# FFN-out by seven block products, two FFN-in tiles read at once, and block sums kept in DRAM

## The chip, the cores and the metric

One core of one Trainium2 chip runs one layer of a sequence model on 512 tokens of width 1024, batch 1, in float32. The metric is the device time of one execution in microseconds. TensorE is called PE, VectorE DVE, ScalarE ACT, GpSimd POOL; SP and POOL issue the DMA transfers spoken of here. Matrix products are exact to about float32: every operand is split into a high part (float32r, cast by ACT) and a low part (the rest, subtracted by DVE), and every product is three matmuls, high by high, high by low, low by high.

## The reference, cut to what matters

```python
def reference(x, ...):                       # x: (1, 512, 1024), D_FF = 2816
    h = rms_norm(x, norm1_g)
    proj = h @ w_in                          # three token mixers and three gate groups
    ...
    branch_out = einsum('blnc,ncd->blnd', branches, w_branch)
    merged = sum(gates * branch_out, axis=2)
    x = x + merged @ w_out                   # 1024 x 1024
    h2 = rms_norm(x, norm2_g)
    gu = h2 @ w_ffn_in                       # 1024 x 5632
    x = x + (silu(gu[..., :D_FF]) * gu[..., D_FF:]) @ w_ffn_out   # 2816 x 1024
    return x
```

The change touches the last two products and the order of the loads ahead of them.

## The kernel before

Activations lie transposed: features on the 128 partitions, the 512 tokens along the free axis. The input projection, the mixers and the gates take the first 545 us or so and are the same in both kernels. Behind them stand four stages.

**Branch merge** (up to about 612 us). For each of eight feature tiles, three products with `w_branch`, multiplied by the gates that SP fetches back from DRAM. Weights of all plain products come 128x512 at a time ("a piece", 256 KB) into a ring `wr` of three tiles (`Dense.load`, L1228), are cast to `wh` by ACT (L1229) and the rest goes to `wl` on DVE (L1230); `wh` and `wl` are rings of six.

**Out-projection** (612 to 664 us). Eight tiles of `w_out`. Behind each tile `take_res` adds the residual (L1717, DVE), `SevenProducts.take` makes the normed input of the FFN and its block sums (L1339 to L1350), `norm.add` adds squares, and the new residual is stored to DRAM (L1720).

**FFN-in** (to 885.8 us). The class `SevenProducts` does the gate and the up product by a Strassen-Winograd scheme over 2 x 2 blocks: the feature axis is cut in two halves of four 128-row tiles, the tokens in two halves of 256, and the weight blocks are the gate and the up column. Instead of eight block products it needs seven, p1 to p7, each of 4 x 3 matmuls of 256 columns (L1391). A tile of 128 gate and 128 up columns costs 84 matmuls; there are 22 tiles, 1848 matmuls in all. They run in pairs, the pieces of the two tiles alternating: p1 p1 p5 p5 p6 p6 p3 p3 p7 p7 p2 p2 p4 p4. Each tile has its own banks, uses half of each, and its results are read by itself: copies of the banks p1, p5, p6, p7 (ACT), additions of 256 columns (DVE), a 512-wide product with the RMS scale (L1443) and SiLU (L1444), and a split of the 512-wide result to `act` (ACT L256, DVE L257).

Of a tile's four weight blocks g0, s, g1, u1, SP loads each (L1377), POOL adds one on top of s and later one on top of g0 (L1375, DMAs that accumulate), and DVE adds g0 and then g1 to s (L1415). The raw blocks lie in a ring of twelve: six tiles that are taken from the slots of the out-projection, which come free late, three new tiles `sp_raw0` to 2, and the three of `wr`. `run` makes a piece (sum, cast, subtract) five pieces ahead of its matmuls: behind the matmuls of piece i in program order come its bank's reads, and ahead of them the split of piece i+5.

**FFN-out** (to 1005.3 us). Plain products: eight tiles of 22 x 3 = 528 matmuls of 512 columns in all (L1301 to L1303). Behind each tile `take_out` multiplies by the RMS scale (L1751), adds the residual read back from DRAM (L1752), and stores the tile (L1753).

The engines run their own instruction streams in program order and wait on semaphores; a scheduler orders the instructions of one stream by readiness in its own estimate when the program is built, so rows of one engine differ somewhat from the code's order.

## Time and profile before

| | us |
|---|---|
| median of 3 runs | 1011.73 |
| lowest, highest | 1007.13, 1014.23 |
| profiled execution, its own time | 1011.66 |
| span in its trace | 1009.9 |
| PE busy | 970.1 (96%) |
| DVE busy | 754.3 (75%) |
| ACT busy | 473.5 (47%) |

The span runs from the first to the last instruction on the core; 1.8 us of the execution's own time lie outside it. Busy shares are averages over stages of different kinds, so that the profile has to be read by stage: a window's row gives each engine's busy time and number of instructions in a stretch, the TensorE clock that was granted, the mean busy share of the 16 DMA engines and the rate. The records of a few matmuls are missing from the trace.

### The profile page before, as it was taken

How to read it: one execution, taken by the hardware profiler on the slowest of the kernel's cores; microseconds unless marked ns; L12 is line 12 of the kernel's file. 1: busy time of each engine (PE TensorE's matmuls, PEld its weight loads, DVE VectorE, ACT ScalarE, POOL GpSimd, SP SyncE). 2: the span in 40 equal slices, each digit the busy share in tenths (PEclk: the TensorE clock that was granted, in tenths of full speed). 3: DMA queues.
4: the chain of work that ended last, by engine and by line, in shares of the span. 5: the costliest groups of instructions: out<-in, count | busy, mean ns of one | idle time of the engine just before them, and what ended most of it. 6: DMA issues, size and time to landing. Idle time of an engine off the chain costs nothing.

```text
span 1009.9 us, 17883 instructions
## 1 busy us (share of the span) xinstructions
PE 970.1 (96%) x6416; PEld 824.2 (82%) x6416; DVE 754.3 (75%) x1941; ACT 473.5 (47%) x978; POOL 143.3 (14%) x176
## 2 busy tenths in 40 slices
PE   7989999899999999999999999989999999999998
PEld 5777777676779777888887788879999999988886
DVE  6899676789994789977867655679989998943331
ACT  6534333434342566446446324566666666632220
POOL 2021120422420001000000332011211221000000
PEclk9999899999998999999999999999999999999999
DMA  7325242221431334252448864476776677354440
GB/s 241 116 53 133 64 110 78 84 56 53 100 96 40 95 105 116 84 156 75 154 149 270 273 194 159 138 178 165 151 163 175 152 153 170 79 155 123 131 136 27
DMA packets 105593, 129.95 MB, mean 129 GB/s; under 512 B 45376, under 2 KB 47296, under 8 KB 105504
## 3 DMA queue, kind: packets, MB, share of 16 engines
q1 hardware_dynamic: 99168, 117.28, 38.7%
q0 software_dynamic: 6336, 11.54, 7.4%
q8 instruction: 50, 0.82, 0.3%
q14 instruction: 39, 0.32, 0.1%
HBM read 109.90 MB, written 18.88 MB: 128 GB/s over the span
## 4 chain that ended last, share of the span: by engine, by line
PE 77%; DVE 15%; DMA 3%; ACT 2%; issue 2%; POOL 1%; SPq 0%; DVEq 0%; ACTq 0%; POOLq 0%
PE bank L1391 21%; PE bank L1302 13%; PE bank L1303 13%; PE bank L1301 13%; DVE wl L1230 2%; DMA ar<-in_w_ffn_in 1%; DMA ar<-ymix 1%; PE bank L468 1%; PE bank L479 1%; PE bank L1188 1%; PE bank L262 1%; PE bank L630 1%; PE bank L1285 1%; PE bank L1286 1%; PE bank L1287 1%
## 5 line engine op out<-in xcount | busy, mean ns | idle before, releaser
L1229 ACT CAST wh<-wr 128x512 fp32r<-128x512 f32 x198 | 120.4, 611 | 208.8 <-PE bank L1302 163.6
L1230 DVE TENSOR_TENSOR wl<-wr,wh 128x512 fp32r<-128x512 f32 x198 | 136.8, 693 | 82.8 <-ACT wh L1229 82.3
L1301 PE MATMUL bank<-act_hi,wh 128*128 128x512 f32 x360 | 150.5, 418 | 7.8 <-ACT wh L1229 5.9
L1302 PE MATMUL bank<-act_lo,wh 128*128 128x512 f32 x360 | 149.7, 416 | 0.8 <-DVE act_lo L257 0.7
L1303 PE MATMUL bank<-act_hi,wl 128*128 128x512 f32 x360 | 149.6, 416 | 0.0
L1391 PE MATMUL bank<-sp_t,wh 128*128 128x256 f32 x528 | 97.5, 285 | 1.1 <-ACT ar L1423 0.8
L1391 PE MATMUL bank<-act_hi,wh 128*128 128x256 f32 x352 | 98.0, 278 | 0.0
L1391 PE MATMUL bank<-act_hi,wl 128*128 128x256 f32 x352 | 97.7, 278 | 0.1
L1391 PE MATMUL bank<-act_lo,wh 128*128 128x256 f32 x352 | 97.5, 277 | 0.0
L1301 PEld LDWEIGHTS bank<-act_hi,wh 128*128 128x128 f32 x360 | 70.0, 195 | 22.7 <-ACT wh L1229 5.9
L1391 PEld LDWEIGHTS bank<-sp_t,wh 128*128 128x128 f32 x528 | 82.7, 193 | 1.5 <-ACT ar L1423 1.0
L1302 PEld LDWEIGHTS bank<-act_lo,wh 128*128 128x128 f32 x360 | 70.0, 194 | 16.4 <-DVE act_lo L257 3.5
L1303 PEld LDWEIGHTS bank<-act_hi,wl 128*128 128x128 f32 x360 | 70.0, 194 | 14.4 <-issue 0.6
L1391 PE MATMUL bank<-sp_t,wl 128*128 128x256 f32 x264 | 75.2, 285 | 0.0
L1301 PE MATMUL bank<-act,wh 128*128 128x512 f32 x176 | 68.5, 389 | 0.0
L1302 PE MATMUL bank<-act,wh 128*128 128x512 f32 x176 | 68.5, 389 | 0.0
L1303 PE MATMUL bank<-act,wl 128*128 128x512 f32 x176 | 68.5, 389 | 0.0
L1391 PEld LDWEIGHTS bank<-act_hi,wl 128*128 128x128 f32 x352 | 66.2, 188 | 0.7 <-DVE wl L254 0.7
L1391 PEld LDWEIGHTS bank<-act_hi,wh 128*128 128x128 f32 x352 | 66.4, 189 | 0.3
L1391 PEld LDWEIGHTS bank<-act_lo,wh 128*128 128x128 f32 x352 | 66.4, 189 | 0.0
L253 ACT CAST wh<-ar 128x512 fp32r<-128x512 f32 x79 | 48.2, 622 | 28.1 <-DMA ar<-in_w_ffn_in 18.1
L254 DVE TENSOR_TENSOR wl<-ar,wh 128x512 fp32r<-128x512 f32 x79 | 53.1, 685 | 9.4 <-ACT wh L253 8.9
(491 smaller groups left out, 2217.7 us busy)
## 6 DMA issues: line engine op xcount, KB each, us to landing
wr<-in_w_in SPq DMA_DIRECT2D x88, 256.0 KB, 2.9
ar<-in_w_ffn_in SPq DMA_DIRECT2D x46, 256.0 KB, 3.2
wr<-in_w_ffn_out SPq DMA_DIRECT2D x40, 256.0 KB, 2.7
gate<-ar SPq DMA_DIRECT2D x24, 256.0 KB, 2.4
wr<-in_w_branch SPq DMA_DIRECT2D x24, 256.0 KB, 3.6
ar<-gate SPq DMA_DIRECT2D x24, 256.0 KB, 3.6
ar<-in_w_ffn_in POOLq DMA_DIRECT2D x22, 256.0 KB, 3.9
sp_raw<-in_w_ffn_in SPq DMA_DIRECT2D x21, 256.0 KB, 3.4
```

The source lines that it names most:

```text
L253: nc.scalar.copy(hi, src)
L254: nc.vector.tensor_tensor(lo, src, hi.bitcast(F32), ALU.subtract)
L262: self.nc.tensor.matmul(ps[:, b, :], sq[:, b * P:(b + 1) * P], self.c("sel"), start=True, stop=True)
L468: nc.tensor.matmul(pa[:, c * P:(c + 1) * P], kb[rows, 4 * q + c].rearrange("p a t -> p (a t)"), ar[rows, 4 * q + c].rearrange("p a t -> p ...
L479: nc.tensor.matmul(pt[64:128, w], aam[q][0:64, c, h, 1], uv[0:64, 4 * q + c, h * CH:(h + 1) * CH], start=True, stop=True)
L630: nc.tensor.matmul(pu[:, 0:P], yt[:, c0:c0 + 2].rearrange("p c t -> p (c t)"), ts, start=True, stop=True)
L1229: nc.scalar.copy(wh, raw)
L1230: nc.vector.tensor_tensor(wl, raw, wh.bitcast(F32), ALU.subtract)
L1301: nc.tensor.matmul(ps, wh[:, j], hi(k), start=k == 0, stop=False)
L1302: nc.tensor.matmul(ps, wh[:, j], lo(k), start=False, stop=False)
L1303: nc.tensor.matmul(ps, wl[:, j], hi(k), start=False, stop=k == nk - 1)
L1391: nc.tensor.matmul(ps, w[x][:, c], b(y, j), start=first and j == js[0] and n == 0, stop=last and j == js[-1] and n == 2, skip_group_check= ...
```

## The change

1. **FFN-out by seven products.** The 22 k-tiles of the activations become two halves of 11, the tokens two halves of 256, and the output columns are taken in two groups of four tiles, g = 0 and 1. A group has three units, over 4, 4 and 3 k-tiles (chunks c); its seven banks accumulate over the three. 2 x 2 x 7 x 11 x 3 = 924 matmuls of 256 columns take the place of 528 of 512. The results of a group are read behind its third unit only, by DVE and ACT for two output tiles at once (`unit_out`), with the scale and the residual.
2. **Two tiles of FFN-in in one bank.** A pair of tiles is one unit; its two products lie in the two halves of a bank and are read by instructions of 512 columns. SiLU and the split are 1024 wide.
3. **Block sums of the activations.** Behind a unit's results DVE makes four block sums of 256 columns; one stays in SBUF, three are written to DRAM (384 KB per unit) and read back by `fetch` for FFN-out, 512 KB (or 384 KB) at a time, twelve times, through the two work buffers `k[1]` and `n[1]`, and split there by ACT and DVE.
4. **Raw blocks** lie in a ring of eleven: `sp_raw0` to 7, new tiles of their own, and the three of `wr`. No slot of the out-projection is used. The second s of a unit is loaded apart from the other head blocks, when piece 8 of the unit before is made.
5. `w_ffn_in` and `w_ffn_out` are arranged by blocks ahead of the launch, `x2dr` is one DRAM tile, the RMS scale has a place of its own.

```diff
@@ SevenProducts.__init__
-        self.raws, self.turn = None, 0
+        self.raws = [E.spool.tile([P, KB * P], F32, name=f"sp_raw{i}") for i in range(8)] + dense.rings["wr"][0]
+        self.turn = 0
+        a = [x for x, _ in E.tail]
+        self.k = [x[:, 0:5 * self.N].rearrange("p (s n) -> p s n", n=self.N) for x in a[0:2]]
+        self.n = [a[2][:, i * 2 * T:(i + 1) * 2 * T].rearrange("p (s n) -> p s n", n=self.N) for i in range(2)]
+        self.sums = a[0][:, 5 * self.N:8 * self.N].rearrange("p (s n) -> p s n", n=self.N)
+        self.sdr = E.dpool.tile([3, P, KF // 2, self.N], F32, name="sp_sums")
...
@@ FFN-in, reads of a unit (two tiles; releases of banks left out)
+        def r2():
+            V.tensor_tensor(ka, ka, bank("p2"), ALU.add)
+            for k, t in ((ka, a), (kb, b)):
+                V.tensor_tensor(k, k, self.R[:, t].unsqueeze(1).broadcast_to([P, 2, N]), ALU.mult)
+            nc.scalar.activation(K[:, 0:4], K[:, 0:4], AF.Silu)
+        def r4():
+            V.tensor_tensor(ka, ka, bank("p1"), ALU.mult)
+            V.tensor_tensor(kb, kb, nb, ALU.mult)
+            V.tensor_tensor(K[:, 4], K[:, 1], K[:, 0], ALU.subtract)
+            V.tensor_tensor(S[:, 1], K[:, 3], K[:, 0], ALU.subtract)
+            V.tensor_tensor(S[:, 0], K[:, 3], K[:, 4], ALU.add)
+            V.tensor_tensor(S[:, 2], S[:, 0], K[:, 2], ALU.subtract)
+            E.split(K[:, 1:5].rearrange("p s n -> p (s n)"), arenas[j][:, 0:4 * N], arenas[j][:, 4 * N:8 * N], -1.0)
+            nc.sync.dma_start(self.sdr[:, :, j].rearrange("s p n -> p s n"), S)
...
+    def fetch(self, i, c):
+        t = (self.k[1], self.n[1])[self.fetched % 2][:, 0:k]
+        nc.sync.dma_start(t, self.sdr[i, :, 4 * c:4 * c + k])
+        hi, lo = self.place(i, c)
+        E.split(t.rearrange("p s n -> p (s n)"), hi[:, 0:k * N], lo[:, 0:k * N], 1.0 if i == 0 else -1.0)
...
@@ FFN-out, reads of a group (r7 without the releases of banks; r1, r5, r6, r2, r4 in the same manner)
+        def r7():
+            V.tensor_tensor(na, kb, bank("p7"), ALU.add)
+            V.tensor_tensor(kb, kb, nb, ALU.add)
+            V.tensor_tensor(kb, kb, bank("p3"), ALU.add)
+            V.tensor_tensor(nb, nb, na, ALU.add)
+            for v, xx, t, sign, q in ((kb, x[0][:, :, 1], b, 1.0, 0), (nb, x[1][:, :, 1], b, -1.0, 1)):
+                scaled(v, t, sign)
+                V.tensor_tensor(v, v, xx, ALU.add)
+                done(v, q, t)
...
+    HEAD, FOURTH = (("g0", 0), ("s", 0), ("g0", 1)), ("s", 1)
+    REST = (("g1", 0), ("u1", 0), ("g1", 1), ("u1", 1))
...
@@ run
+                if k % n == 0 and k:
+                    self.fill(k // n, *self.REST)
+                    self.fill(k // n + 1, *self.HEAD)
                 pieces[k][0]()
+                if k % n == 8:
+                    self.fill(k // n + 1, self.FOURTH)
...
+    for u, k, i, c in ((n - 1, 1, 0, 0), (n - 1, 4, 1, 0), (n - 1, 6, 2, 0), (n, 0, 0, 1), (n, 2, 1, 1), (n, 6, 2, 1),
+                       (n + 1, 0, 0, 2), (n + 1, 2, 1, 2), (n + 1, 6, 2, 2), (n + 2, 6, 2, 0), (n + 3, 6, 2, 1),
+                       (n + 4, 6, 2, 2)):
+        between.setdefault(14 * u + 2 * k + 1, []).append(lambda i=i, c=c: sp.fetch(i, c))
-    for d in range(KD):
-        dense(A["w_ffn_out"][d], KF, lambda k: ah[k], lambda k: al[k], take_out(d))
```

How instructions move is shown at three places.

SP's stream in the branch merge before (L1228 loads weights, L1695 fetches gates, L1377 loads raw blocks of FFN-in), just behind `sp_raw0` and 1:

```order
L1377 DMA sp_raw2_5979<-in_w_ffn_in 128x512
L1695 DMA ar13_14_82<-gate_60_270 128x512
L1228 DMA wr_16_102<-in_w_branch 128x512
L1695 DMA ar12_13_81<-gate_68_278 128x512
L1228 DMA wr_19_114<-in_w_branch 128x512
L1695 DMA ar12_13_81<-gate_52_262 128x512
L1228 DMA wr_22_135<-in_w_branch 128x512
L1695 DMA ar11_12_80<-gate_61_271 128x512
L1228 DMA wr_16_102<-in_w_branch 128x512
```

The other raw blocks of the first pairs stand further down in that stream, behind the loads of the out-projection:

```order
L1377 DMA wr_19_114<-in_w_ffn_in 128x512
L1720 DMA x2_207_5676<-ar13_14_82 128x512
L1377 DMA ar12_13_81<-in_w_ffn_in 128x512
L1377 DMA ar13_14_82<-in_w_ffn_in 128x512
L1720 DMA x2_208_5677<-ar13_14_82 128x512
L1377 DMA ar12_13_81<-in_w_ffn_in 128x512
L1377 DMA ar11_12_80<-in_w_ffn_in 128x512 x2
```

The same place of the merge in the changed kernel (L1234 weights, L1809 gates, L1382 raw blocks):

```order
L1382 DMA sp_raw2_5674<-in_w_ffn_in 128x512
L1382 DMA sp_raw3_5675<-in_w_ffn_in 128x512
L1234 DMA wr_16_102<-in_w_branch 128x512
L1809 DMA ar13_14_82<-gate_60_270 128x512
L1382 DMA sp_raw4_5676<-in_w_ffn_in 128x512
L1382 DMA sp_raw5_5677<-in_w_ffn_in 128x512
L1234 DMA wr_19_114<-in_w_branch 128x512
L1809 DMA ar12_13_81<-gate_68_278 128x512
L1809 DMA ar12_13_81<-gate_52_262 128x512
L1382 DMA sp_raw6_5678<-in_w_ffn_in 128x512
L1234 DMA wr_22_135<-in_w_branch 128x512
L1382 DMA sp_raw7_5679<-in_w_ffn_in 128x512
```

All eight raw blocks of the first unit, in eight tiles of their own, are now loaded within the merge.

ACT's stream at the end of FFN-in before (L1229 casts pieces of FFN-out, L1436 copies a bank, L1444 is SiLU, L256 casts the result):

```order
L1229 CAST wh_211_5990<-wr_19_114 128x512
L1436 COPY ar11_12_80<-bank5_88 128x256
L1229 CAST wh_17_103<-wr_22_135 128x512
L1436 COPY ar11_12_80<-bank1_84 128x256
L1229 CAST wh_20_115<-wr_16_102 128x512
L1444 ACTIVATE ar12_13_81<-ar12_13_81 128x512
L1229 CAST wh_23_137<-wr_19_114 128x512
L1229 CAST wh_25_143<-wr_22_135 128x512
L1444 ACTIVATE ar13_14_82<-ar13_14_82 128x512
L256 ACTIVATE act_223_6054<-ar12_13_81 128x512
L1229 CAST wh_27_148<-wr_16_102 128x256
L256 ACTIVATE act_223_6054<-ar13_14_82 128x512
```

ACT's stream in the last FFN-in unit of the changed kernel (L259 casts a piece, L1479 and L1456 copy banks, L262 to `sp_t0` or `act_hi` casts a fetched sum, L1464 is SiLU):

```order
L1479 COPY ar11_12_80<-bank3_86 128x2x256
L259 CAST wh_25_143<-wr_16_102 128x512
L262 ACTIVATE sp_t0_5668<-ar13_14_82 128x1024
L259 CAST wh_27_148<-wr_22_135 128x512
L259 CAST wh_203_5989<-sp_raw0_5672 128x512
L259 CAST wh_17_103<-sp_raw2_5674 128x512
L1456 COPY ar13_14_82<-bank3_86 128x512
L259 CAST wh_20_115<-sp_raw1_5673 128x512
L259 CAST wh_23_137<-sp_raw3_5675 128x512
L262 ACTIVATE act_hi_91<-ar12_13_81 128x1024
L262 ACTIVATE act_hi_91<-ar13_14_82 128x1024
L1464 ACTIVATE ar11_12_80<-ar11_12_80 128x1024
```

Three of the casts of fetched sums stand here among those of the pieces, and a fourth, of the first fetch, in the row just ahead of the L1479 copy; two stand ahead of SiLU.

DVE's stream at the end of FFN-out before (L1230 makes a piece, L1751 and L1752 are the results of a tile):

```order
L1230 TENSOR_TENSOR wl_18_104<-wr_22_135,wh_17_103 128x512
L1230 TENSOR_TENSOR wl_21_116<-wr_16_102,wh_20_115 128x512
L1230 TENSOR_TENSOR wl_24_140<-wr_19_114,wh_23_137 128x512
L1230 TENSOR_TENSOR wl_26_144<-wr_22_135,wh_25_143 128x512
L1751 TENSOR_TENSOR ar11_12_80<-bank5_88,ar12_13_81 128x512
L1230 TENSOR_TENSOR wl_28_149<-wr_16_102,wh_27_148 128x256
L1752 TENSOR_TENSOR ar12_13_81<-ar12_13_81,ar11_12_80 128x512
L1751 TENSOR_TENSOR ar13_14_82<-bank1_84,ar12_13_81 128x512
L1752 TENSOR_TENSOR ar13_14_82<-ar13_14_82 128x512
```

DVE's stream in the changed kernel where group 0 ends and group 1 begins (L1546 to L1562 read results of group 0, L260 makes a piece):

```order
L260 TENSOR_TENSOR wl_21_116<-sp_raw3_5675,wh_20_115 128x512
L1547 TENSOR_TENSOR ar11_12_80<-ar11_12_80,bank5_88 128x2x256
L1549 TENSOR_TENSOR ar13_14_82<-ar13_14_82 128x2x256
L1521 SCALAR_TENSOR_TENSOR ar11_12_80<-ar11_12_80,ar12_13_81 128x2x256
L1521 SCALAR_TENSOR_TENSOR ar13_14_82<-ar13_14_82,ar12_13_81 128x2x256
L1552 TENSOR_TENSOR ar11_12_80<-ar11_12_80,ar12_13_81 128x2x256
L1552 TENSOR_TENSOR ar13_14_82<-ar13_14_82 128x2x256
L1556 TENSOR_TENSOR ar11_12_80<-ar11_12_80,bank2_85 128x2x256
L1521 SCALAR_TENSOR_TENSOR ar13_14_82<-ar13_14_82,ar12_13_81 128x2x256
L1521 SCALAR_TENSOR_TENSOR ar11_12_80<-ar11_12_80,ar12_13_81 128x2x256
L1562 TENSOR_TENSOR ar13_14_82<-ar13_14_82 128x2x256
L1559 TENSOR_TENSOR ar11_12_80<-ar11_12_80,ar12_13_81 128x2x256
L260 TENSOR_TENSOR wl_24_140<-sp_raw5_5677,wh_23_137 128x512
```

Eleven result instructions of 512 columns stand in a row between the third and the fourth piece of group 1; at the end of the program the same results (15 instructions with those around them) are DVE's last rows.

## Rows read from the trace of the kernel before

**Rows 1.** The profile's page: busy time of each engine, and the chain that ended last.

```profile
PE 970.1 (96%) x6416; PEld 824.2 (82%) x6416; DVE 754.3 (75%) x1941; ACT 473.5 (47%) x978; POOL 143.3 (14%) x176
PE 77%; DVE 15%; DMA 3%; ACT 2%; issue 2%; POOL 1%; SPq 0%; DVEq 0%; ACTq 0%; POOLq 0%
```

**Rows 2.** Busy time by window: length, engines, granted clock, DMA share, GB/s.

```profile
650.00:676.00 26.00, 21.73 (x125) 18.65 (x124) 20.65 (x43) 15.89 (x35) 5.39 (x6) 0.98 0.69 167
695.00:855.00 160.00, 160.00 (x1376) 159.82 (x1375) 144.54 (x276) 102.98 (x212) 27.81 (x32) 1.00 0.70 162
890.00:1000.00 110.00, 110.00 (x487) 91.09 (x486) 34.92 (x55) 24.07 (x41) 0.00 (x0) 1.00 0.40 120
```

**Rows 3.** The chain of waits from 640 us: start, length, what.

```profile
661.18 4.40 DMA ar<-in_w_ffn_in
...
675.00 10.28 PE bank L1391 x73
...
885.76 0.23 PE bank L1301
...
1005.24 0.24 PE bank L1303
```

**Rows 4.** What PE waited for, 640 to 690 us: total, times, longest.

```profile
PE bank L1303 <- DVE wl L1230: 2.0, 1, 2.0
PE bank L1542 <- DVE ar L1529: 1.2, 1, 1.2
PE bank L1391 <- ACT ar L1423: 0.8, 1, 0.8
PE bank L1391 <- ACT ar L1429: 0.2, 1, 0.2
```

**Rows 5.** PE by window at the start of FFN-in: busy, count, granted clock, DMA.

```profile
674.00:676.00 2.00, 1.77 (x12) 0.77 0.36 41
676.00:678.00 2.00, 2.00 (x11) 0.50 0.83 186
678.00:680.00 2.00, 2.00 (x17) 0.88 0.84 238
```

**Rows 6.** The casts of FFN-in's results: the second one (timeline), all 22 (by tile).

```profile
692.36 0.64 ACT L256 ACTIVATE act<-ar 128x512 fp32r<-128x512 f32 x1 [0.84 <-DVE ar L1450]
...
L256 ACT ACTIVATE act<-ar x22: 616/632/635, 690.5 to 886.9; 128x512 fp32r<-128x512 f32 x22
```

**Rows 7.** DVE groups by shape in FFN-in, 695 to 855 us: busy, mean ns, idle.

```profile
L254 DVE TENSOR_TENSOR wl<-ar,wh 128x512 fp32r<-128x512 f32 x60 | 40.3, 684 | 4.8 <-ACT wh L253 4.4
...
L1438 DVE TENSOR_TENSOR ar<-ar 128x256 f32<-128x256 f32 x16 | 6.7, 418 | 0.0
...
L1415 DVE TENSOR_TENSOR ar<-ar,ar 128x512 f32<-128x512 f32 x9 | 6.1, 681 | 0.0
```

**Rows 8.** DVE's timeline in the out-projection: start, length, instruction.

```profile
658.39 0.68 DVE L1717 TENSOR_TENSOR ar<-ar,bank 128x512 f32<-128x512 f32 x1
658.99 0.68 DVE L1230 TENSOR_TENSOR wl<-wr,wh 128x512 fp32r<-128x512 f32 x1
```

**Rows 9.** ACT groups by shape, 695 to 855 us.

```profile
L1444 ACT ACTIVATE ar<-ar 128x512 f32<-128x512 f32 x16 | 10.1, 633 | 12.6 <-DVE ar L1443 12.6
L1426 ACT COPY ar<-bank 128x256 f32<-128x256 f32 x17 | 6.2, 365 | 0.1
```

**Rows 10.** DMA issues of the page: queue, count, KB each, median us to landing.

```profile
sp_raw<-in_w_ffn_in SPq DMA_DIRECT2D x21, 256.0 KB, 3.4
...
sp_raw<-in_w_ffn_in POOLq DMA_DIRECT2D x10, 256.0 KB, 4.2
...
ar<-in_w_lora SPq DMA_DIRECT2D x1, 512.0 KB, 5.8
```

**Rows 11.** The timeline at the end of the program.

```profile
1005.08 0.39 PE L1303 MATMUL bank<-act,wl 128*128 128x512 f32 x1
1005.51 0.69 DVE L1751 TENSOR_TENSOR ar<-bank,ar 128x512 f32<-128x512 f32 x1 [13.33 <-PE bank L1303]
1006.23 0.69 DVE L1752 TENSOR_TENSOR ar<-ar 128x512 f32<-128x512 f32 x1
```

More of the change, by code (lines that the diff above doesn't have):

```diff
@@ L1378, in load @@
         return t
-    def split(self, w):
-        d = self.dense
-        hi, lo = d.ring("wh", F32R, WB[1] + 1), d.ring("wl", F32R, WB[1] + 1)
-        self.E.split(w, hi, lo)
-        return hi, lo
-    def matmuls(self, ps, w, b, js, first, last):
-        nc = self.E.nc
-        for j in js:
-            c = slice(j * P, (j + 1) * P)
-            for n, (x, y) in enumerate(((0, 0), (0, 1), (1, 0))):
-                nc.tensor.matmul(ps, w[x][:, c], b(y, j), start=first and j == js[0] and n == 0,
-                                 stop=last and j == js[-1] and n == 2, skip_group_check=True)
@@ L1413, in sum_ @@
-        def sum_(other, after=None):
-            def f():
-                V.tensor_tensor(o["s"], o["s"], o[other], ALU.add)
-                if after:
-                    after()
-                return o["s"]
-            return f
+        K, Nn, S = self.k[j % 2], self.n[j % 2], self.sums
+        ka, kb, na, nb = K[:, 1:3], K[:, 0:4:3], Nn[:, 0:2], Nn[:, 2:4]
+        u = dict(blocks=blocks, h=H, banks={}, own=False, new=True, last=True)
+        bank = lambda name: u["banks"][name].rearrange("p (t n) -> p t n", n=N)
@@ new lines, in unit_out, with block, fill @@
+        u["read"] = dict(p1=r1, p5=r5, p6=r6, p7=r7, p2=r2, p4=r4)
+        return u
+    def block(self, u, i, t):
+        w = u["blocks"][i]
+        n = w.shape[1] // 2
+        return w[:, t * n:(t + 1) * n]
+    def fill(self, i, *keys):
+        if i < len(self.units):
+            u = self.units[i]
+            for name, t in keys:
+                u[name, t] = self.load(self.block(u, dict(g0=0, s=1, g1=3, u1=2)[name], t))
+            for name, t in keys:
+                if name == "s":
+                    self.load(self.block(u, 2, t), u["s", t])
@@ new lines, with begin, run @@
+    HEAD, FOURTH = (("g0", 0), ("s", 0), ("g0", 1)), ("s", 1)
+    REST = (("g1", 0), ("u1", 0), ("g1", 1), ("u1", 1))
+    def begin(self, units):
+        self.units, self.fetched = units, 0
+        self.pieces = [p for u in units for p in self.seven(u)]
+        self.fill(0, *self.HEAD, self.FOURTH, *self.REST)
+        for k in range(self.FIRST):
+            self.pieces[k][0]()
+    def run(self, norm, between):
+        pieces, made, n = self.pieces, self.FIRST, 14
+        self.fill(1, *self.HEAD)
@@ L1522, in add @@
         with E.scope("s"):
-            sq = E.slot("rsq", keep=True)
+            sq = self.into if self.into is not None and self.n == 0 else E.slot("rsq", keep=True)
             E.nc.scalar.activation(sq, x, AF.Square)
@@ L1547, in __call__ @@
             nc.tensor.transpose(pb[:, b * P:(b + 1) * P], w[:, b * P:(b + 1) * P], E.ident)
-        E.free(w, pss)
+        E.free(*([pss] if self.into is not None else [w, pss]))
         return pb
```

272 lines of the change are left out of this document (155 added, 117 removed).

## The prediction

> **What bounds the kernel now.** I read the page first, then the chain of waits, then the windows by stage. The page shows PE busy for 96% of the span and on 77% of the chain that ended last [rows 1]. The windows say that this holds stage by stage: in steady FFN-in PE is busy for all 160 us at full clock, in FFN-out for all 110 [rows 2]. So a matmul less is time less, so long as nothing else becomes late. What could is DVE: 144.5 of 160 us in FFN-in, but only 34.9 of 110 in FFN-out [rows 2]. The one place where PE is not full is the start of FFN-in, 650 to 676 us, with 21.7 of 26 us. There the chain runs through loads of `w_ffn_in`, of which the longest shown holds it for 4.4 us [rows 3], and PE's waits are 2.0, 1.2, 0.8 and 0.2 us [rows 4]. Behind them the granted clock falls to 0.50, the lower of its two levels (1.2 GHz against 2.4), for one window and part of the next two [rows 5]. The program ends with two DVE instructions and a store behind the last matmul [rows 11].
>
> The sum is made against the profiled execution, 1011.66 us, which stands at the median of the runs, 1011.73.
>
> **1. Matmuls of FFN-out: -12.7.** Before: from 885.76 to 1005.47 (the last start plus 0.23) is 119.7 us for 528 matmuls, 0.2267 each [rows 3]. Their price at 256 columns comes from FFN-in: the casts of the second tile of the first and of the last pair start at 692.4 and 886.9, ten units of 168 matmuls later, so 19.45 us a unit and 0.1158 each [rows 6]. 924 x 0.1158 = 107.0. Ends: half of a 512-column one (0.1133) gives 104.7, the 1376 records in 160 us, some missing, give 0.1163 and 107.4 [rows 2]. So -12.2 to -15.
>
> **2. The start of FFN-in: -4.5.** The four waits sum to 4.2 us. In 674 to 680 us PE ran 40 matmuls where 52 would fit at 0.1158; less the 0.2 of waiting this is 1.2 us of clock. Together 5.4. The raw blocks of the first pairs came late since six of their tiles were slots of the out-projection: SP issued them behind its stores. Now eight tiles are free from the merge on, and SP's rows put all eight loads there. What may stay is the way from the last residual through gain, block sums and splits on ACT and DVE to p6 and the RMS matmul (the 1.2 of L1542): four pieces of 12 matmuls, 5.6 us, lie beside it. I leave 0.9. Ends: 0, if that way was the real cause, to -5.4. For the five loads that move ahead of weights and gates in SP's queue during the merge, +0.5 (0 to +1): each is 3.4 us of transfer [rows 10], the ring of three weight tiles being the cover; if that cover is gone, a weight is late by one such load in part.
>
> **3. Steady FFN-in: 0.** By durations of DVE, two tiles took 14 splits and 4 sums at 0.68, twelve reads of 256 columns at 0.42, two scalings and two results at 0.68 [rows 7], 20.1 us. Now: the same splits and sums, 7 reads at 0.68, 4 sums of 256 at 0.42, and a 1024-wide result, 1.22 by adding 0.27 for each 256 columns as between the shapes of these rows: 20.0. ACT: four copies of 365 ns less by pairing, and SiLU and cast of 1024 wide at about 1.17 for pairs of 633 [rows 9]: no more than before. DVE starts instructions 0.60 apart that last 0.68 [rows 8], which is how 20.1 fits in 19.45; what hides all this is PE, and the margin is below 2 us a unit. The stores of sums add 0.4 MB to a unit at a DMA share of 0.70 [rows 2]; nobody waits for them there. Ends: 0, and the second rival.
>
> **4. From FFN-in to FFN-out: +3 (0 to +7).** The fetches work through two buffers that the unit before the last still uses. The first is issued once that unit's results are split, about 5.5 us into the last unit, and takes as long as the nearest transfer of its size, 512 KB in 5.8 us [rows 10]. In ACT's order its cast stands ahead of the copy of p6, ready at six pieces, 8.3 us: ACT, with five casts of pieces queued behind, stands for some 3 us. Five pieces ahead are 7 us of cover, so PE need not see it. The next two fetches stand ahead of SiLU in the same way, and behind SiLU wait the products and p6's split of the first FFN-out unit, with some 4 us left. Thirdly, DVE gets three splits of 1024 more in a unit and a half, 27.9 us of work on 27.6 us of PE. I take 2.5 for this border, and 0.5 for the fetches of the other units, whose buffers are free early.
>
> **5. From group 0 to group 1: +4.2 (+2 to +7).** From the end of p7, DVE has in its order 15 results, 7 splits and 4 sums to the split with which p3 of group 1 can start. Independent ones start 0.60 apart [rows 8], those on the result before 0.72 (1005.51 to 1006.23) [rows 11]: 15 x 0.66 + 11 x 0.605 = 16.6 us. PE has four pieces of 9 matmuls and six of 12 in that time, 12.5. The difference is 4.1, and 0.1 for the step from matmul to DVE. The VectorE page of the Trainium skill (VectorE: DVE Perf Modes, section The DRAIN you can't avoid) says that a next operation does not start until the pipe has emptied, and itself excepts operations that are not held; by that the 26 would cost their durations, 17.8, and this term +5.3. The starts 0.60 apart speak for the lower price. A stall of several us may also take the clock: before, PE's waits at FFN-in's start ended in 1.2 us lost [rows 4, 5], and that is in the upper end. The Trainium skill (TensorE: Matmul & The Clock Gate, section HAM oscillation — how this bites in real kernels) lets gaps of PE that recur lower the clock each time. It speaks against a change that makes two new gaps; at the row's price that would be 2.4 us for both. I count none in the sum, since the wait of 2.0 us alone did not bring the clock down: 0.98 over 650 to 676 us is what the 0.77 of the last two leaves [rows 2, 5].
>
> **6. The tail: +4.3 (+3.5 to +5.5).** Before, 1.45 us of DVE lie behind the last matmul's end (1005.47 to 1006.92) [rows 11]. After, 15 results of 512 columns follow p7's end, 15 x 0.66 = 9.9, beside 4 pieces x 9 x 0.1158 = 4.2 us of PE: 5.7 behind the last matmul. The store that follows is as before.
>
> Sum: -12.7 - 4.5 + 0.5 + 0 + 3 + 4.2 + 4.3 = -5.2: **1006.5 us**. Its own range, from terms 2, 4 and 5, is 1002 to 1011.
>
> **Rivals.**
> - *The borders are cheap.* The start gives all 5.4, the extra loads nothing, FFN-in ends with 0.5, and 2 and 3.5 are paid at the other borders: 1011.66 - 12.7 - 5.4 + 0.5 + 2 + 3.5 = 999.6. For it: PE has five pieces ahead, and DVE is two thirds idle in plain FFN-out. Against it: DVE's order at the group's end is fixed, and shows eleven results in a row.
> - *s comes late in every unit: slower.* With eleven raw tiles the second s of a unit takes the tile of this unit's first g0, which is free only with p7's split, about 7.5 us into the unit. The load (3.4) and the accumulation (4.2) [rows 10] need 7.6; ACT wants it for p5's cast 16.6 us in, and about 1.1 more can be hidden: it decides when they need over 10.3. At one and a half times these rows, 11.4, each of ten units loses 1.1, 11 in all: 1006.5 + 11 = 1017.5. For it: the DMA share is 0.70 already and rises. Against it: the rows are medians of just this stage.
> - *The fetches choke FFN-out of group 0.* Its units move some 4 MB in 19.5 us, 215 GB/s, against 162 in FFN-in [rows 2]. If weights and fetches come late by half a us for each of the nine fetches, 4.5: 1011, no change. The same time results if the change does not do what it does at the start, because the chain there was not the loads (-4.5 gone).
>
> **How the numbers follow.** Chances: the forecast 0.48, cheap borders 0.25, choking or no gain at the start 0.15, late s 0.09, other 0.03. A measurement of this kernel can tell about 1%, 10 us, from no change: faster means below 1001.6, slower above 1021.9. Faster: nearly all of the cheap case and a little of the forecast's low end, 0.30. Slower: a third to a half of the late s (it may cost more than 11) and what I have not thought of, 0.09. Within: 0.61. The range leaves out one in ten on either side: from 996.5, cheap borders with matmuls at their lower end, to 1017, just at the late s.
>
> **What would show it.** FFN-out's matmuls at 0.116 on average; no PE waits on DVE or ACT between 655 and 675 us, and full clock there; in the timeline a PE gap before p5 and p3 of group 1 with DVE as releaser, of 4 us in all; 15 DVE rows at the end, the last about 6 us behind the last matmul; at the border of the stages PE waits below 7 us. It would be wrong if PE waited in every unit of FFN-in, if the fetches' landing took well over 6 us, or if PE showed no wait at the group's border.

## The result, and the profile after

The changed kernel is slower by 0.8%: median 1016.32 us of 20 runs (1011.51 to 1021.13) against 1007.95 of 20 for the kernel before (1004.82 to 1015.65), ratio 1.0079, 95% interval 1.0059 to 1.0099. On another chip the ratio was 1.0109 (1.0083 to 1.0135). The forecast was 1006.5, 5 us less than the 1011.66 of the profiled execution before.

The two profiled executions must not be compared as wholes. Up to the first branch matmul both kernels have the same instructions, yet the one takes 431.6 us and the other 423.7: before, the granted clock was 0.97, 0.96 and 0.91 in 120 to 160, 160 to 200 and 280 to 320 us, and after, 1.00 in all three. From there on the stages differ as follows, here with the main experiments. The column merge starts at the first branch matmul, and other work of the mixers lies in it; the out-projection starts at 617.6 us before (not at 612). FFN-in runs from the end of the out-projection to the first matmul on `act`, FFN-out to the end of the last matmul, the tail to the end of the span; all in us, from one profiled execution of each kernel. The ratio is that of all executions.

| kernel | merge | out-proj. | FFN-in | FFN-out | tail | sum | ratio to before (95%) |
|---|---|---|---|---|---|---|---|
| before | 186.0 | 46.0 | 222.0 | 119.7 | 4.6 | 578.3 | |
| changed | 187.2 | 44.1 | 221.8 | 126.6 | 8.9 | 588.6 | 1.0079 (1.0059-1.0099) |
| e1_order | 187.0 | 44.1 | 223.6 | 120.1 | 8.9 | 583.7 | 1.0028 (0.9997-1.0059) |
| e2_nofetch | 187.1 | 44.2 | 221.0 | 121.0 | 8.7 | 581.9 | 1.0011 (0.9977-1.0044) |
| e3_copyfirst | 187.5 | 44.1 | 222.9 | 127.9 | 8.9 | 591.3 | 1.0091 (1.0056-1.0126) |
| e4_early | 185.9 | 44.1 | 222.9 | 124.5 | 7.0 | 584.4 | 1.0035 (1.0012-1.0058) |
| e7_copies | 187.2 | 44.1 | 218.1 | 127.0 | 9.0 | 585.4 | 1.0069 (1.0034-1.0103) |
| e8_fetches | 187.9 | 44.1 | 219.8 | 122.1 | 9.0 | 582.8 | 1.0021 (0.9996-1.0046) |
| e10_noresult | 187.5 | 44.1 | 223.3 | 116.0 | 8.9 | 579.8 | one run |
| e9_all | 186.6 | 44.2 | 219.3 | 120.7 | 7.0 | 577.8 | 0.9983 (0.9956-1.0011) |
| e14_defer2 | 187.4 | 44.2 | 216.5 | 125.2 | 7.0 | 580.3 | 1.0015 (0.9986-1.0044) |
| e16_fetch_early | 187.7 | 44.1 | 222.7 | 115.2 | 7.0 | 576.7 | 0.9934 (0.9907-0.9961) |

So FFN-out, which the change was to shorten by 12.7 us of matmuls, is 6.9 us longer.

The units of FFN-out in which PE does not wait show the price of a matmul there. The second unit of group 0 of the changed kernel, 168 matmuls, runs from the first of these rows to the second, 19.84 us or 0.1181 each:

```profile
904.42 0.39 PE L1424 MATMUL bank<-act,wh 128*128 128x256 f32 x2
...
924.26 0.39 PE L1424 MATMUL bank<-act,wh 128*128 128x256 f32 x2
```

At that price the 924 matmuls are 109.1 us. The rest of FFN-out, 17.5 us, lies in two units alone: the first unit of group 0 takes 27.58 us, 7.7 more than 19.84, and the first unit of group 1 29.57, 9.7 more.

The page of the changed kernel, busy time and chain (against [rows 1]): PE does fewer columns, DVE more instructions, and PE's share of the chain falls from 77 to 65%.

```profile
PE 958.2 (95%) x6812; PEld 832.6 (82%) x6812; DVE 814.0 (80%) x1985; ACT 499.8 (49%) x964; POOL 164.2 (16%) x200
PE 65%; DVE 19%; DMA 7%; ACT 4%; issue 3%; POOL 1%; SPq 0%; ACTq 0%; DVEq 0%; POOLq 0%
```

In the windows of the changed kernel the start of FFN-in, where PE had been busy for 21.73 of 26 us [rows 2], is full. Two places are new: 880 to 900, in the first unit of group 0, and 940 to 960, in the first unit of group 1.

```profile
650.00:676.00 26.00, 25.91 (x199) 24.82 (x200) 24.13 (x56) 17.54 (x33) 2.58 (x3) 1.00 0.55 145
700.00:860.00 160.00, 158.78 (x1350) 157.22 (x1349) 145.12 (x242) 97.80 (x161) 27.70 (x32) 1.00 0.75 179
880.00:900.00 20.00, 15.47 (x106) 14.56 (x105) 15.11 (x24) 10.26 (x16) 1.73 (x2) 0.83 0.69 183
940.00:960.00 20.00, 13.61 (x91) 12.93 (x90) 13.88 (x24) 6.21 (x11) 2.62 (x3) 0.83 0.85 226
```

The next rows show what PE waited for in the changed kernel from 600 us to the end (total, times, longest), and the two longest waits in its timeline. Both are ahead of p3, which follows p6:

```profile
PE bank L1424 <- ACT wh L259: 8.9, 3, 4.7
PE bank L1424 <- DVE wl L260: 2.0, 3, 1.1
PE bank L1424 <- ACT ar L1479: 1.7, 1, 1.7
PE bank L1424 <- ACT ar L1478: 1.0, 4, 0.5
```

```profile
890.77 0.80 PE L1424 MATMUL bank<-act,wh 128*128 128x256 f32 x2 [3.64 <-ACT wh L259]
...
954.92 0.80 PE L1424 MATMUL bank<-act,wh 128*128 128x256 f32 x2 [4.72 <-ACT wh L259]
```

The chain of the changed kernel at the start of group 1 shows DVE's results running without a break to 944.2, then a split of p5 and p6's sum (L1401). POOL's accumulating DMA, which adds to g0 for p7, may go out only when p6's sum has read g0; from its issue to its landing it takes 7.1 us:

```profile
943.60 0.14 DVE ar L1559
943.74 0.46 issue
944.20 0.68 DVE wl L260
944.88 0.61 DVE sp_raw L1401
...
946.03 7.08 DMA sp_raw<-in_w_ffn_out
...
953.74 1.14 ACT wh L259 x2
```

ACT's timeline in the same place shows it standing for 5.8 us at that DMA. Of the casts that follow at once, five in 2.8 us, the third and fourth are p3's:

```profile
946.80 0.62 ACT L259 CAST wh<-sp_raw 128x512 fp32r<-128x512 f32 x1 [0.58 <-DVE sp_raw L1401]
953.21 2.78 ACT L259 CAST wh<-sp_raw 128x512 fp32r<-128x512 f32 x5 [5.79 <-DMA sp_raw<-in_w_ffn_out]
```

ACT's stream says why p3 waits for p7's transfer. Behind p6's two casts stand those of `sp_raw2` (p7) and `sp_raw6` (p2), and only then p3's; this order is the scheduler's, by its own estimate of readiness. In group 0 p7's two casts stand ahead of p3's as well.

```
L259 CAST wh_25_143<-sp_raw3_5675 128x512
L259 CAST wh_27_148<-sp_raw5_5677 128x512
L259 CAST wh_20_115<-sp_raw2_5674 128x512
L259 CAST wh_25_143<-sp_raw6_5678 128x512
L259 CAST wh_203_5989<-sp_raw3_5675 128x512
L259 CAST wh_17_103<-sp_raw5_5677 128x512
```

PE's own stream has the same order in part. At the start of group 1 only two matmuls of p3 stand ahead of the first six of p7 (moving operand `sp_t`), and the other 22 of p3 follow these. So at this border a p3 cast in time would have given PE two matmuls before it stopped at p7. The rows go on from the wait at 954.92:

```profile
955.52 0.63 PE L1424 MATMUL bank<-sp_t,wh 128*128 128x256 f32 x2
...
956.80 0.41 PE L1424 MATMUL bank<-act,wl 128*128 128x256 f32 x1
```

Behind each of the two stops the granted clock is 0.50, the lower of its two levels, for a while. Windows of 4 us of the changed kernel, PE (a count takes in a matmul at either edge):

```profile
888.00:892.00 4.00, 1.23 (x4) 0.57 0.73 225
892.00:896.00 4.00, 4.00 (x23) 0.58 0.72 218
952.00:956.00 4.00, 1.08 (x5) 0.68 0.98 282
956.00:960.00 4.00, 4.00 (x21) 0.50 0.84 265
960.00:964.00 4.00, 4.00 (x34) 0.97 0.94 238
```

By their starts, PE began 25 matmuls from 890.77 to 896, where 44.3 fit at 0.1181, and 56 from 954.92 to 964, where 76.9 fit: 2.3 and 2.5 us lost.

### The profile page after: what moved, and what is told of

Its sections match the earlier page's. It is cut to its first block, busy times and chain, and to the rows that moved or that the text cites. A ratio compares the mean times of both kernels' runs of the same rounds, so it can differ in the third digit from the quotient of the medians.

```text
span 1012.3 us, 18842 instructions
## 1 busy us (share of the span) xinstructions
PE 958.2 (95%) x6812; PEld 832.6 (82%) x6812; DVE 814.0 (80%) x1985; ACT 499.8 (49%) x964; POOL 164.2 (16%) x200
## 4 chain that ended last, share of the span: by engine, by line
PE 65%; DVE 19%; DMA 7%; ACT 4%; issue 3%; POOL 1%; SPq 0%; ACTq 0%; DVEq 0%; POOLq 0%
PE bank L1424 21%; PE bank L1308 9%; PE bank L1309 9%; PE bank L1307 9%; DVE wl L260 2%; DVE wl L1236 2%; DMA ar<-ymix 1%; DMA ar<-sp_sums 1%; PE bank L474 1%; DMA wr<-in_w_ffn_in 1%; PE bank L1194 1%; DMA sp_raw<-in_w_ffn_in 1%; PE bank L485 1%; PE bank L268 1%; PE bank L636 1%
## 5 line engine op out<-in xcount | busy, mean ns | idle before, releaser
L1235 ACT CAST wh<-wr 128x512 fp32r<-128x512 f32 x150 | 92.3, 620 | 120.0 <-PE bank L1308 80.0
L259 ACT CAST wh<-sp_raw 128x512 fp32r<-128x512 f32 (+1 forms) x172 | 101.8, 611 | 91.9 <-PE bank L1424 51.2
L260 DVE TENSOR_TENSOR wl<-sp_raw,wh 128x512 fp32r<-128x512 f32 (+1 forms) x172 | 112.6, 674 | 33.0 <-ACT wh L259 29.6
L1424 PE MATMUL bank<-act_hi,wl 128*128 128x256 f32 x440 | 122.1, 278 | 1.0 <-DVE wl L260 1.0
L1424 PE MATMUL bank<-act_hi,wh 128*128 128x256 f32 x440 | 122.3, 278 | 0.5 <-ACT wh L259 0.5
L1424 PE MATMUL bank<-act_lo,wh 128*128 128x256 f32 x440 | 121.9, 277 | 0.0
L1236 DVE TENSOR_TENSOR wl<-wr,wh 128x512 fp32r<-128x512 f32 x150 | 106.3, 711 | 13.0 <-ACT wh L1235 12.5
L1424 PE MATMUL bank<-act,wh 128*128 128x256 f32 x352 | 67.3, 292 | 8.4 <-ACT wh L259 8.4
L1424 PEld LDWEIGHTS bank<-act,wh 128*128 128x128 f32 x352 | 57.3, 200 | 8.8 <-ACT wh L259 8.8
L1424 PEld LDWEIGHTS bank<-sp_t,wl 128*128 128x128 f32 x308 | 59.3, 193 | 0.0
```

Source lines behind the costliest of these rows:

```text
L259: nc.scalar.copy(hi, src)
L260: nc.vector.tensor_tensor(lo, src, hi.bitcast(F32), ALU.subtract)
L1235: nc.scalar.copy(wh, raw)
L1236: nc.vector.tensor_tensor(wl, raw, wh.bitcast(F32), ALU.subtract)
L1424: E.nc.tensor.matmul(ps[:, t * self.N:(t + 1) * self.N], w[a][:, c], x(b, j), start=first and t == 0 and j == 0 and i == 0, stop=u["last"] ...
```

## The experiments

**e1_order**: each cast of FFN-out's pieces is kept behind the cast of the piece before (order of issue only). The helper that adds this order is left out here.

```diff
+                cast = E.split(x[:, 0:n], hi, lo)
+                if u["own"]:
+                    if self.cast is not None:
+                        E.behind(cast, self.cast)
+                    self.cast = cast
```

> One edit of the changed kernel: in FFN-out ACT casts the pieces in the order in which TensorE uses them (p3 ahead of p7; before, the scheduler had put p7's cast ahead of p3's at the start of both groups). Theory ORDER (ACT stands at p7's cast until an accumulating DMA has landed that is issued only behind p6's sum, and p3, ready long before, is queued behind it): the PE gaps ahead of p3 of the first unit of group 0 and of group 1 (3.6 and 4.7 us) shrink by about the 2.8 us of the two p3 pieces, the low clock behind them shrinks or goes, and FFN-out from its first to its last matmul falls from 126.7 us to 117 to 121. Theory DVE (the prediction's: DVE's results and sums at the border set the gap by themselves): DVE's work is the same, so FFN-out stays within 1.5 us of 126.7.

FFN-out took 120.1, so ORDER holds. PE's order changed with ACT's: at the start of group 1 p3's 24 matmuls now stand whole ahead of p7's, so the run shows the worth of both orders together. ACT's timeline there has p3's second cast at 949.46 and p7's first, which waits for the DMA, behind it:

```profile
949.46 0.62 ACT L259 CAST wh<-sp_raw 128x512 fp32r<-128x512 f32 x1 [0.26 <-PE bank L1435]
952.65 0.62 ACT L259 CAST wh<-sp_raw 128x512 fp32r<-128x512 f32 x1 [2.57 <-DMA sp_raw<-in_w_ffn_out]
```

At the start of group 1 six small waits of 3.4 us in all were left, 2.9 of them for DVE's `wl`, and the clock stayed at 1.00 (940 to 964):

```profile
PE bank L1435 <- DVE wl L260: 2.9, 5, 1.7
PE bank L1435 <- ACT wh L259: 0.5, 1, 0.5
```

In group 0 waits of 0.5, 0.4, 1.3 and 0.5 us were left, and the clock fell to 0.63 (892 to 896).

**e2_nofetch**: the line `nc.sync.dma_start(t, self.sdr[...])` of `fetch` is left out.

> The changed kernel without the twelve transfers that bring the parked sums back (the casts and subtractions of the fetches stay, and work on what lies in the buffers, so the sums are not those of the reference). Theory FETCH (late fetches hold ACT at the end of FFN-in and through it SiLU, the last unit's results and the sums of FFN-out's first unit): PE's 1.7 us wait for p6's copy in the last FFN-in unit goes (FFN-in 221.8 to about 220), the 4.5 us of PE waits at the start of FFN-out and the low clock behind them go, so FFN-out falls from 126.7 to about 120; the waits at the start of group 1 (6.4 us in all) stay. Theory DVE: the waits at the start of FFN-out stay above 3 us, as DVE has the same work.

FFN-out took 121.0, and the wait for p6's copy was gone. The waits at the start of group 0 went from 4.5 to 2.8 us only, so the fetches are some two fifths of them. The waits at the start of group 1 did not stay: they were 5.5 us, in other places: 2.2 ahead of p7, whose first matmuls the scheduler had put ahead of half of p6's, and 1.6 ahead of p3, at a clock of 1.00. Of the 5.6 us by which FFN-out fell, 2.7 came in that unit, where the order of PE and ACT had changed along with the fetches. FFN-in gained 0.8, not 1.7: the pairs before lost some more to copies than in the changed kernel's profile.

**e3_copyfirst**: in FFN-in the result's split (`E.split` of 1024) is traced in the next pair's `r1`, its cast behind that copy.

> One edit of the changed kernel: in FFN-in ACT copies bank p1 of the next pair ahead of the 1024-wide cast of this pair's result, not behind it. Theory COPY (that cast waits on DVE's last products, the copy is queued behind it, and p6, which adds into the same bank, waits for the copy): a pair of FFN-in takes 19.5 us and not 19.96, FFN-in falls from 221.8 to 217 to 218.5. Theory PITCH (256-column matmuls into two halves of one bank, or the busier DMA, are slower by themselves): pairs stay at 19.9 to 20.0 and FFN-in at 221 to 222.

FFN-in did not fall (222.9). From p4 to p6 the time was back at 8.32 us, but p3 now waited for p5's copy, which stood behind the same cast, 2.7 us in five places. So I took both copies:

**e7_copies**: the same, in `r5`.

> One edit of the changed kernel: in FFN-in ACT makes the copies of both banks p1 and p5 of the next pair ahead of the 1024-wide cast of this pair's result (the run before, with p1's copy alone ahead of it, had brought the stretch from p4 to p6 from 8.6 to 8.32 us and in exchange made p3 wait for p5's copy, which stood behind the cast). Theory COPY: neither p6 nor p3 waits for a copy in the ten full pairs, a pair takes 19.5 to 19.65 us, and FFN-in falls from 221.8 to 218 to 219.5; a part may be lost again in the last pair, where the buffer for the first fetch comes free later. Theory PITCH (two halves of a bank, busier DMA): 19.9 and 221 to 223 as before.

FFN-in took 218.1. Nearly every pair took 19.52 us, as before the change (over nine pairs 19.58 on average, against 19.91 in the changed kernel and 19.56 before). One p6 to the next, in the timelines of the kernel before, of the changed one and of e7:

```profile
734.07 0.39 PE L1391 MATMUL bank<-sp_t,wh 128*128 128x256 f32 x2
753.59 0.39 PE L1391 MATMUL bank<-sp_t,wh 128*128 128x256 f32 x2
```

```profile
801.20 0.51 PE L1424 MATMUL bank<-sp_t,wh 128*128 128x256 f32 x2 [0.19 <-ACT ar L1478]
821.16 0.50 PE L1424 MATMUL bank<-sp_t,wh 128*128 128x256 f32 x2 [0.16 <-ACT ar L1478]
```

```profile
777.86 0.39 PE L1431 MATMUL bank<-sp_t,wh 128*128 128x256 f32 x2
797.38 0.39 PE L1431 MATMUL bank<-sp_t,wh 128*128 128x256 f32 x2
```

19.52, 19.96 and 19.52: COPY holds, PITCH does not. The total did not show it (1.0069, 1.0034 to 1.0103).

**e4_early**: in `unit_out` the four operations of the half `kb` move from `r7` to an `r3`, and two of `na` from `r2` to `r7`.

> One edit of the changed kernel: in FFN-out the four result operations of DVE that need neither p7 nor p2 are done behind p3 (and the rest regrouped, with the same number of operations), so that 11 and not 15 stand behind p7. Expected by all theories: the stretch from the last matmul to the end falls from 8.7 us by 2.4 to about 6.3. At the group border, theory ORDER: p6's sums and with them the accumulating DMA come about 2.4 us earlier, and the gap ahead of p3 falls from 4.7 to about 2.3. Theory DVE says much the same of the sum of the three waits (6.4 to about 4). If the gap stays at 4.7, the transfer is late for a reason of its own.

The tail took 7.0 us, a fall of 1.9. The waits at the start of group 1 fell from 6.4 to 3.9, but not as expected: none is left ahead of p3, and the long one stands ahead of p7, whose first two matmuls the scheduler has put ahead of half of p6's:

```profile
950.28 0.80 PE L1424 MATMUL bank<-sp_t,wh 128*128 128x256 f32 x2 [2.98 <-ACT wh L259]
```

The transfer took 4.9 us here and not 7.1. So the order and the transfer changed together with the delay, and this run alone does not show what the delay costs.

**e8_fetches**: fetch (0, 0) is traced behind p6's read, the third to fifth fetch are traced later too, and the third and fourth fetch's casts stand behind SiLU.

> The changed kernel with ACT's work on the first fetches moved: the first behind the copy of p6, the third and fourth behind SiLU of the last pair. Theory FETCH: PE's 1.7 us wait for p6's copy goes (FFN-in 221.8 to about 220), SiLU, the last products and p6's sum of FFN-out come some 2 us earlier, and the waits at the start of group 0 (4.5 us) fall to 1 to 3; FFN-out 126.7 to 122 to 125. In a rival (the transfer that adds to p7's weights, not the fetches, is late at the start of group 0) only the 1.7 us go, and the gap ahead of p3 stays at 3 us or more.

FFN-in took 219.8; the 1.7 us went, and at the start of group 0 2.5 us were left of 4.5: FETCH holds, in part. Group 1 kept its long wait (4.8 us), and FFN-out took 122.1.

**e10_noresult**: for g = 0, `r7`, `r2` and `r4` free their banks and store, and do nothing else.

> The changed kernel without the eleven result operations of DVE behind p7, p2 and p4 of group 0 (half of the output is then not the reference's; the banks are freed and the stores made as before). ACT's order at that border is then the order of use, as in the run with casts in order, so the two are compared. If DVE's results are what is left there in that run (waits of 3.4 us in 6 places between 940 and 958 us), these waits go, and FFN-out falls from the changed kernel's 126.7 to about 117 to 118 (4.7, 1.7 and the low clock of the second border gone). If the accumulating transfers set it by themselves, PE still waits 2 us or more for ACT ahead of p7 or p3 of group 1.

FFN-out took 116.0; at the start of group 1 PE did not wait at all. The same window as above, 940 to 960, in this kernel:

```profile
940.00:960.00 20.00, 20.00 (x172) 20.00 (x171) 13.51 (x21) 9.88 (x17) 2.77 (x4) 1.00 1.02 297
```

So the transfer into p7's weights, which took 7.5 us here, is in time when p6's sums are and p3 stands ahead of p7, at a DMA share of 1.02. The first unit of group 1 took 19.84 us, the price without any wait.

**e9_all**: e1, e4, e7 and e8 together.

> All order edits together on the changed kernel: casts of FFN-out in piece order, both copies ahead of the cast in FFN-in, the first fetches moved behind p6's copy and SiLU, and the four early results of FFN-out. By the sum of the single edits' stage times (casts in order -6.5 in FFN-out; early results -1.9 in the tail and up to -2 at the border; copies about -3 in FFN-in; fetches about -2) 11 to 13 us less than the changed kernel, so about 1004 beside a kernel before of 1007: ratio to before 0.994 to 1.000. If the stalls were only symptoms of DVE being full, the edits overlap and the ratio stays above 1.000.

The ratio is 0.9983, level with the kernel before. The edits overlap: 4.6 us of waits were left at the start of group 1, the longest 1.7 ahead of p7, with low clock behind it (0.74 in 948 to 952).

**e11_p2** and **e12_defer**: p2 ahead of p7 in FFN-out; e12 also defers results of group 0.

> The run with all order edits, and in FFN-out p2 now stands ahead of p7, so that the transfer that adds to p7's weights behind p6's sum has six pieces and not four (8.3 us and not 5.6) until p7 needs it. Theory TRANSFER (what is left at the borders is this transfer, 7.2 us at the start of group 1): the 1.7 us wait ahead of p7 of group 1 goes and the low clock behind it, FFN-out falls from 120.7 to 116 to 118. Theory DVE (its 15 results): the waits for the weights of p1, p5 and p6 of group 1 (2.8 us in five places) stay in either case, and if FFN-out stays within 1 us of 120.7, they were all.

> The run before in this list, and the results of p2, p7 and p4 of group 0 are done among the first pieces of group 1 (behind the fourth, sixth and eighth piece) and no longer ahead of them; the banks allow it. Theory DVE: the waits at the start of group 1 all go, as in the run without these results, and FFN-out is 112 to 115; ratio to the kernel before 0.988 to 0.995. If weights are late there for another reason (transfers), PE still waits 2 us or more for ACT ahead of p5 or p6 of group 1.

Both failed by my edit and say nothing on their question. The second s of the next unit is loaded when piece 8 is made; with p2 there, the tile of the first g0 was filled anew ahead of p7, so that p7 had other weights than the reference's and waited for that load (6.6 us in e11). Ratios 1.0116 (1.0092 to 1.0140) and 1.0110 (1.0073 to 1.0148).

**e13_after_again**: the changed kernel.

> The changed kernel itself, as it stands, on the chip of the two others: a ratio to the kernel before of 1.005 to 1.011, FFN-in 221 to 224 (its single edits left between 221.0 and 223.6 where they did not touch it), FFN-out 125 to 128, tail 8.7 to 9.

It came out as expected: ratio 1.0109 (1.0083 to 1.0135), FFN-in 222.7, FFN-out 125.6, tail 8.9.

**e14_defer2**, **e15_order_defer**: p7 stays ahead of p2; results of group 0 behind pieces 4, 6 and 8 of group 1, in e9's kernel and in the changed one with casts in order and early results.

```diff
+        if g == 0:
+            for name, i in (("p2", 3), ("p7", 5), ("p4", 7)):
+                u["read"][name] = lambda f=u["read"][name], i=i: self.later.append((i, f))
```

> The run with all order edits (pieces of FFN-out in their old order, p7 ahead of p2), and the results of p7, p2 and p4 of group 0 are done behind the fourth, sixth and eighth piece of group 1 and no longer ahead of them. Theory DVE (the results at the border delay p6's sums, these the transfer into p7's weights): the six waits at the start of group 1 (4.6 us) and the low clock behind them go, as in the run without these results, and FFN-out falls from 120.7 to 113 to 116; ratio to the kernel before 0.989 to 0.996. Theory TRANSFER (the accumulating transfer is late there by itself): PE still waits 1.5 us or more ahead of p7 of group 1, and FFN-out stays at 118 to 121.

> The FFN-out edits alone on the changed kernel: casts in piece order, early results, results of group 0 deferred; FFN-in and the fetches as they were. By the stage times FFN-in 221.5 to 224, the waits at the start of group 0 as in the run with casts in order (3 to 4 us), none above 0.6 us at the start of group 1, FFN-out 115 to 118, tail 7; total about 3 us above the other kernel of this pair.

Of the waits up to p7 of group 1 only 1.1 and 1.4 us were left, but 1.6 and 1.3 came further on, in the next unit's p1, and the fetch for p4, which I had moved behind the results since they hold its buffer, came late, and the time went there: FFN-out took 125.2 and 125.5, ratios 1.0015 and 1.0102 (1.0058 to 1.0146). e14's timelines, PE and ACT:

```profile
958.99 0.58 PE L1437 MATMUL bank<-act_hi,wh 128*128 128x256 f32 x1 [6.46 <-ACT act_hi L262]
```

```profile
957.88 1.06 ACT L262 ACTIVATE act_hi<-ar 128x1024 fp32r<-128x1024 f32 x1 [6.64 <-DMA ar<-sp_sums]
```

**e16_fetch_early**: that fetch through `k[1]`, free with p2's results, which come ahead of p7's.

> The run with the deferred results, but the first fetch of group 1 goes through the other work buffer, free with p2's results, and is issued behind the fourth piece of group 1 (with the deferred results it had waited for their residual's buffer, landed at 957.9 and kept p4 waiting for 6.5 us). p2's results are done ahead of p7's, which they don't need. Expected: the 6.5 us wait ahead of p4 and the low clock behind it go, no wait above 1.6 us in FFN-out, which falls from 125.2 to 113 to 117; tail 7; ratio to the kernel before 0.988 to 0.996. If the fetch is late again (over 9 us from issue to landing, as SP's queue stands at it), p4 waits 2 us or more and the ratio stays above 0.997.

FFN-out took 115.2, and the ratio to the kernel before is 0.9934 (0.9907 to 0.9961): 0.7% faster than it, clear of the noise. 940 to 960 has 1.7 us of waits and full clock:

```profile
940.00:960.00 20.00, 18.27 (x147) 1.00 0.81 195
```

FFN-in took 222.7 in this profile and 216.5 in e14's, with the same instructions in the same order there. The difference lies at four places where PE waits for a bank's copy, 3.8 us of waits and what followed them. At the longest, 1.9 us, ACT stood at a cast whose block of `w_ffn_in` had not landed, with the copy of p5's bank next in its order; in e14 the same cast did not wait:

```profile
865.49 0.62 ACT L259 CAST wh<-sp_raw 128x512 fp32r<-128x512 f32 x1 [2.83 <-DMA sp_raw<-in_w_ffn_in]
```

Why the block lands later in some executions is open.

Across the runs FFN-out's loss lies at the two borders. This is the time of each group's first unit beyond 19.84 us:

| kernel | group 0 | group 1 |
|---|---|---|
| changed | 7.7 | 9.7 |
| e1_order | 5.7 | 5.3 |
| e2_nofetch | 4.8 | 7.0 |
| e4_early | 7.9 | 7.5 |
| e8_fetches | 3.6 | 9.3 |
| e10_noresult | 6.9 | 0.0 |
| e9_all | 2.2 | 8.3 |
| e16_fetch_early | 2.2 | 2.9 |

## Why the prediction was wrong

The steps, with what was predicted and what the profiles and runs gave:

| step | predicted | measured |
|---|---|---|
| 1 matmuls of FFN-out | -12.7 | -10.6 (924 x 0.1181) |
| 2 start of FFN-in, merge | -4.5, +0.5 | -1.9 in the out-projection, -4.9 to p4 of the first pair, merge +1.2 |
| 3 steady FFN-in | 0 | +3.1 (copies) |
| 4 FFN-in to FFN-out | +3 | +9.4: 1.7 of wait for a copy, and 7.7 in the first unit of group 0 |
| 5 group 0 to 1 | +4.2 | +9.7 in the first unit of group 1 |
| 6 tail | +4.3 | +4.3 |
| sum | -5.2 | +10.3 (single profiles; by the ratio of all executions about 8) |

In the 7.7 us are 4.5 of waits and 2.3 lost behind the longest, in the 9.7 6.4 and 2.5. The rest, under 1 us in each, stands behind the smaller waits: the first matmul behind a stop takes longer (0.39 and more for 0.28). In e1, at a clock of 1.00, the first unit of group 1 lost 5.3 us with 3.4 of waits; why a stop costs so much beyond itself there is open.

**The steps that failed are 5 and 4, by the same wait.** Step 5 reads: "From the end of p7, DVE has in its order 15 results, 7 splits and 4 sums to the split with which p3 of group 1 can start". As a count of DVE's work it was right. In e1, with ACT and PE in order, the first split of p3 ended 16 us behind p7 (predicted 16.6), and the waits there were 3.4 us (predicted 4.1); without the results there were none. In the changed kernel that split came some 21 us behind p7. The sum ended at DVE: I took p3's split to be DVE's next and did not look at where its cast stands on ACT: behind p7's cast, and that behind an accumulating DMA that goes out only with p6's sum and lands 7.1 us later, where its row of the kernel before had a median of 4.2 [rows 10]. Nor does the sum take in PE's order, in which six matmuls of p7 follow the first two of p3. A late sum then costs its own delay plus a transfer. e1 shows what the order costs, 4.4 us of the 9.7. That DVE's results are the delay is shown by e10 (one execution), where the loss is 0.0, and by e16, where they stand behind the first pieces and it is 2.9, against 8.3 in e9, which has the casts in order and the results where they were. All three have p3 ahead of p7, as e1 has. So with the order mended first, the order is worth 4.4 us and the delay the other 5.3; what the delay costs in the old order is not shown, since e4 changed the order too.

**Step 4** missed by more, 9.4 us for 3. It named the wait for the first fetch and dismissed it: "Five pieces ahead are 7 us of cover, so PE need not see it". The copy of p6's bank has no such cover, since p7 adds into the same bank. It stood on ACT behind the cast of the first fetch, and PE waited 1.7 us for it; e8 removed that:

```profile
866.69 1.06 ACT L262 ACTIVATE act_hi<-ar 128x1024 fp32r<-128x1024 f32 x1 [2.04 <-DMA ar<-sp_sums]
```

In the first unit of group 0 the same order as in step 5, p7's cast ahead of p3's, made the wait of 3.64. There the fetches are what makes p6's sums late: with their casts moved in e8 that wait became two of 0.9 and 1.0, and the unit's loss fell from 7.7 to 3.6; with ACT's casts in order in e1 it fell to 5.7, and with both in e9 to 2.2.

**Step 3** compared busy times, which were right (145 us of DVE in 160, as before), and not the order. p6 adds into p1's bank and must wait for its copy; the copy stood on ACT behind a 1024-wide cast that waited for DVE. Before, the copies of two tiles were apart and the casts short. It cost 0.44 us in the pair shown and 0.35 on average, as e7 shows. This is the sign that the prediction had named against itself, PE waiting in every unit of FFN-in: none of the nine pairs took less than 19.73 us.

**The clock** was priced at 1.2 us in step 5 and left out of the sum. The price was too low: in 674 to 680 the windows' counts, 40 matmuls, take in those at the edges, and by the starts 34 ran there, which makes it 1.8 us. In the changed kernel the clock fell behind both long stops, and 2.3 and 2.5 us were lost there. The rule that I set aside, of the Trainium skill (TensorE: Matmul & The Clock Gate, HAM oscillation — how this bites in real kernels), is borne out by these rows: the stops recur, and each is paid again. The 2.0 us wait that I took as proof to the contrary [rows 4] was shorter than either. The length of one wait doesn't decide alone: in e2 a wait of 2.2 us at group 1 left the clock at 1.00, while in e9 it fell behind one of 1.7 with five shorter ones ahead, and in e1's group 0 behind one of 1.3 between three of 0.4 to 0.5.

**Step 1** was mis-sized by 2.1 us: the price of a matmul was taken from FFN-in, where a pair's 168 take 19.52 us (0.1162), and in FFN-out they take 19.84 in every unit without a wait, 0.1181, which lies outside the step's own bounds. Why they are slower there is open.

**Right** were step 6, and step 2 in its direction, with a gain above its own upper end (6.8 us against 5.4; the merge lost 1.2). No run separates the early loads from the rest of the change there. The tail's chain is as counted, 15 DVE operations, the first at 999.42 and the last ending at 1008.89 beside a last matmul at 1003.32; most starts stand 0.60 apart as in [rows 8]. The durations added up whole, as the Trainium skill (VectorE: DVE Perf Modes, The DRAIN you can't avoid) has it for operations that are held, would have been too much here too, 10.3 us for the 9.5 from the first start to the last end:

```profile
999.42 0.69 DVE L1544 TENSOR_TENSOR ar<-ar,bank 128x512 f32<-128x512 f32 x1 [1.18 <-PE bank L1424]
...
1007.49 0.68 DVE L1566 SCALAR_TENSOR_TENSOR ar<-bank,ar 128x512 f32<-128x512 f32 x1
1008.20 0.69 DVE L1568 TENSOR_TENSOR ar<-ar 128x512 f32<-128x512 f32 x1
```

Of the rivals, the late s was not seen as a wait of PE in any full pair. "The fetches choke" came nearest. It was right that fetches are late at the start of group 0, and wrong that weights and fetches come late all through: outside the two first units the matmuls of FFN-out lost nothing, and group 1 lost more than group 0.

## What to carry to other kernels

At a border between stages, follow each engine's order to the end of the chain: a late instruction on one engine costs not its delay alone, but the transfer that may start only behind it, and whatever an in-order engine has queued behind the instruction that waits for that transfer. Being several pieces ahead covers the pieces, not a copy out of a bank that the next product adds to. Where results and preparation share an engine, put the results behind the preparation if the banks allow it; with the six changes of order of e16 the same arithmetic is 0.66% faster than before (0.39 to 0.93%), and not 0.8% slower. And read the order of the engine that computes as well as that of the engine that feeds it: an edit of one may change the other, and the gain is then that of both.
